# Operand distances for split products, and two more places for expert weights

## The chip, the cores and the metric

One core of one Trainium2 chip runs the whole program as one launch. The metric is the device time of that launch in microseconds, the median of several runs. TensorE multiplies, VectorE (DVE), ScalarE (ACT) and GpSimd (POOL) do the elementwise work, and SyncE (SP) issues nearly all large transfers from its queue, in order.

## The reference, cut to what matters

A network on 256 tokens of width 1024, all in float32. Three blocks follow one another: two layers of feed-forward and gated or pooling mixers (each layer has two SwiGLU feed-forwards of inner width 2816); an attention block (two kinds of heads side by side) with a mixture of 32 experts, each token going to 4 of them; and a block with attention and a scan, cross attention to a memory, and a feed-forward with a short convolution. The expert part is, with `h` the normalised tokens:

```python
logits = xf @ w_router + b_router            # 256 x 32
top_val, top_idx = lax.top_k(logits, 4)
gates = jax.nn.softmax(top_val, axis=-1)
hid = xb @ w_mlp1[e] + b_mlp1[e]             # rows of the tokens that chose e; 1024 x 2048
act = glu * sigmoid(1.702 * glu) * (lin + 1) # glu, lin: even and odd columns, clipped
y = act @ w_mlp2[e] + b_mlp2[e]              # 1024 x 1024, weighted by the gate and summed
```

The weights of one expert are 12 MB, those of all 32 are 384 MB.

## The kernel before

Activations lie transposed: `xT` is 128 partitions x 8 x 256, 8 KB in each partition.

**Split products.** Outside the experts a float32 product is made of three products of type fp32r. Each operand is split into a rounded part and the rest (`split`, `norm_parts`), and `mm3` issues high by high, high by low, low by high (L180, L181, L182). The weights, 128 x 128, are the stationary operand (in the profile `LDWEIGHTS`, engine PEld); the activations, 128 x 256, are the moving one. `xhi` and `xlo` hold the split input of a stage, two constant tiles of 8 KB a partition; `ahi`, `alo` (`yhi`, `mhi`, `so`, `ao`, `raw` elsewhere) are split intermediate activations. Split weights lie in tiles `hi` of a ring (`rings`, pool `splitp`, 4 or 8 tiles of 8 KB, high part then low part), in some stages with further tiles on the right side of the memory.

Where things lie follows from the order and the sizes of the pools. The constants begin at byte 16512 of each partition; `xT` is at 17088, `xhi` at 25280, `xlo` at 33472; then come `small`, `rawp` (ten slots of 8 KB for raw weights) from 55840, and the ring from 137760. Tiles inside an operand are multiples of 512 bytes, so what is left is the remainder of the addresses by 512:

| operand | remainder before | minus that of the weights, modulo 512 |
|---|---|---|
| weights in the ring `splitp` | 32 | |
| weights in the right ring (cross attention, convolution) | 480 | |
| `xhi`, `xlo` | 192 | 160 (224 to the right ring) |
| `ahi` of the four feed-forwards; `so`, `ao`, `mhi`; `raw` | 32 | 0 |
| `ahi` of the gated stage (`sgu`) | 64 | 32 |
| `ahi` of the pooling mixer, `yhi` of the cross attention, `ahi` of the convolution stage | 160 | 128 to `splitp`, 192 to the right ring |

**Experts.** `moe` takes the experts in an order that is partly known only after the routing. Expert 0 comes first, and its weights are loaded while the attention still runs. SP then reads the expert's number from `ids` (L1740) and issues 12 loads of 1 MB each (L1264), each into the next place of a fixed turn: 7 slots of `rawp`, 4 places of its own, 3 slots of `rawp`, 14 places. A load waits until the place's last reader is done, and everything behind it on SP's queue waits too.

The rows of the tokens that an expert wants are gathered by a product with a one-hot matrix. The tokens are split: `thi` and `tlo` lie in the memory of `xhi` and `xlo`, written by ACT (L1381) and, for the low part, by VectorE (`lows`, L1386, three pieces before the ranking of the experts and five behind it). Each gather multiplies both with the one-hot matrix `oh` (type fp32r): L1451 for expert 0, L1468 (`dispatch`, from `prepare`) for four places of the order at a time. `xT` stays in its constant tile, untouched, until `post_norm` adds the experts' output to it. Behind the last expert comes a loop for what did not fit (`For_i`, here run zero times), before which all engines meet at a barrier.

The program's order on TensorE is written out by hand in some stages (`in_order`); for the rest, and for SP's queue, a scheduler at build time orders instructions by priority and readiness.

## Time and profile before

| | us |
|---|---|
| median of 3 runs | 2688.53 (2688.33 to 2691.99) |
| the profiled execution, its own time | 2696.91 |
| its span, first to last instruction | 2695.2 |
| TensorE busy | 2443.8 (91%) |
| VectorE / ScalarE / GpSimd busy | 1343.3 / 918.1 / 254.0 |
| moved by DMA | 716.20 MB |

The profiled execution is 8.4 us slower than the median without the profiler. Durations of matrix products in the profile are modelled and overlap: the next one starts before the last has ended, so "busy" says that TensorE has work, not how fast it goes. The stages, by the trace: first feed-forward to 206 us, gated stage to 396, two feed-forwards to 597 and 754, pooling mixer to 850, feed-forward to 1036, attention to about 1196, experts to about 2187, attention and scan to 2400, cross attention to 2496, convolution stage to the end.

### The profile page before, as it was taken

What the parts mean: (1) busy time and instruction counts of PE and PEld (TensorE: products, weight loads), DVE (VectorE), ACT (ScalarE), POOL (GpSimd) and SP (SyncE); (2) the same over time, 40 slices, a digit from 0 to 9 for tenths busy, and PEclk for the clock granted to TensorE, in tenths of its full rate; (3) what the DMA queues carried; (4) which work ended last, traced back from release to release, by engine and by line L of the source; (5) the groups of instructions that cost most, each with busy time, mean ns of one, the idle gap of its engine ahead of it and who ended that gap; (6) DMA issues with size and microseconds to landing.
All of it is one profiled execution on the core that took longest, in us unless ns stands there. A gap on an engine that the chain in (4) does not pass through costs nothing. (4 is left out here: it accounts for less than half of the span.)

```text
span 2695.2 us, 42836 instructions
## 1 busy us (share of the span) xinstructions
PE 2443.8 (91%) x17207; PEld 1863.6 (69%) x17207; DVE 1343.3 (50%) x2786; ACT 918.1 (34%) x1531; POOL 254.0 (9%) x444
## 2 busy tenths in 40 slices
PE   7999999999999999999889888789777787999998
PEld 7998999999999998784333333223222156998997
DVE  5556677577777775942111111111111059766875
ACT  4445454454445444531100100001010042555653
POOL 0011000110021102220000000000000027111000
PEclk8999999999999999999989989899999798999999
DMA  7956455676737652449999999999999973444640
GB/s 240 325 181 201 158 195 196 211 254 219 235 126 266 207 178 97 142 183 367 419 413 420 416 415 418 420 420 419 420 419 419 419 268 110 157 162 136 218 142 17
DMA packets 274116, 716.20 MB, mean 266 GB/s; under 512 B 15023, under 2 KB 179354, under 8 KB 223610
## 3 DMA queue, kind: packets, MB, share of 16 engines
q1 hardware_dynamic: 269370, 703.63, 69.8%
q0 software_dynamic: 4544, 9.80, 1.1%
q8 instruction: 136, 2.23, 0.3%
q14 instruction: 66, 0.54, 0.1%
HBM read 703.84 MB, written 9.54 MB: 265 GB/s over the span
## 5 line engine op out<-in xcount | busy, mean ns | idle before, releaser
L182 PE MATMUL b<-xhi,hi 128*128 128x256 f32 x2392 | 681.5, 285 | 15.7 <-DVE hi L164 15.6
L180 PE MATMUL b<-xhi,hi 128*128 128x256 f32 x2392 | 685.9, 287 | 6.0 <-ACT xhi L192 4.9
L181 PE MATMUL b<-xlo,hi 128*128 128x256 f32 x2392 | 680.8, 285 | 4.6 <-DVE xlo L193 2.4
L164 DVE TENSOR_TENSOR hi<-raw,hi 128x1024 fp32r<-128x1024 f32 (+3 forms) x517 | 605.9, 1184 | 157.5 <-ACT hi L163 152.7
L163 ACT CAST hi<-raw 128x1024 fp32r<-128x1024 f32 (+3 forms) x517 | 509.7, 1003 | 510.4 <-PE b L182 458.4
L180 PEld LDWEIGHTS b<-xhi,hi 128*128 128x128 f32 x2392 | 460.3, 192 | 19.5 <-ACT hi L163 7.8
L182 PEld LDWEIGHTS b<-xhi,hi 128*128 128x128 f32 x2392 | 460.1, 192 | 18.2 <-DVE hi L164 18.0
L181 PEld LDWEIGHTS b<-xlo,hi 128*128 128x128 f32 x2392 | 460.3, 192 | 6.5 <-DVE xlo L193 4.5
L1477 DVE TENSOR_SCALAR g<-b 128x256 f32<-128x256 f32 x48 | 20.3, 422 | 596.1 <-PE b L1496 331.8
L180 PE MATMUL b<-ahi,hi 128*128 128x256 f32 x1072 | 303.4, 284 | 1.8 <-ACT ahi L163 1.7
L181 PE MATMUL b<-alo,hi 128*128 128x256 f32 x1072 | 302.3, 282 | 2.2 <-DVE alo L164 1.3
L182 PE MATMUL b<-ahi,hi 128*128 128x256 f32 x1072 | 301.7, 282 | 0.0
L181 PEld LDWEIGHTS b<-alo,hi 128*128 128x128 f32 x1072 | 203.4, 190 | 3.2 <-DVE alo L164 2.2
L180 PEld LDWEIGHTS b<-ahi,hi 128*128 128x128 f32 x1072 | 203.1, 190 | 3.0 <-ACT ahi L163 2.9
L182 PEld LDWEIGHTS b<-ahi,hi 128*128 128x128 f32 x1072 | 203.5, 190 | 0.0
L1480 ACT ACTIVATE sg<-g 128x256 f32<-128x256 f32 x48 | 20.0, 416 | 525.5 <-DVE g L1477 525.5
L1528 PE MATMUL b<-raw,xe 128*64 128x512 f32 x648 | 153.1, 609 | 16.6 <-DMA raw<-in_w_mlp_dram 16.6
L1496 PE MATMUL b<-raw,xe 128*32 128x512 f32 x928 | 124.9, 650 | 35.3 <-DMA raw<-in_w_mlp_dram 35.0
L1577 ACT COPY y<-b 64x512 f32<-64x512 f32 x68 | 39.4, 579 | 249.4 <-PE b L1570 241.6
L1528 PEld LDWEIGHTS b<-raw,xe 128*64 128x64 f32 x648 | 42.6, 138 | 118.1 <-issue 74.4
L452 DVE TENSOR_TENSOR t<-b,rb 128x256 f32<-128x256 f32 x88 | 37.1, 422 | 167.2 <-PE b L182 167.1
L1496 PEld LDWEIGHTS b<-raw,xe 128*32 128x32 f32 x928 | 24.1, 112 | 118.6 <-DMA raw<-in_w_mlp_dram 75.7
(662 smaller groups left out, 3278.7 us busy)
## 6 DMA issues: line engine op xcount, KB each, us to landing
raw<-in_w_mlp_dram SPq DMA_DIRECT2D x275, 1024.0 KB
wb<-in_w_mlp_dram SPq DMA_DIRECT2D x108, 1024.0 KB
raw<-in_ffn_w_in_dram SPq DMA_DIRECT2D x84, 1024.0 KB
raw<-in_ffn_w_out_dram SPq DMA_DIRECT2D x44, 1024.0 KB
raw<-in_w_ada_dram SPq DMA_DIRECT2D x24, 1024.0 KB
raw<-in_ffn_w_up_dram SPq DMA_DIRECT2D x22, 1024.0 KB
raw<-in_w_in_dram SPq DMA_DIRECT2D x21, 1024.0 KB
raw<-in_a_w_in_dram SPq DMA_DIRECT2D x16, 1024.0 KB
```

What stands on the lines that cost most here:

```text
L163: a = self.nc.scalar.copy(hi, src)
L164: return a.ins, self.nc.vector.tensor_tensor(lo, src, hi.bitcast(F32), op=ALU.subtract).ins
L180: mm(out, whi, xhi, start=start, stop=False, skip_group_check=True)
L181: mm(out, whi, xlo, start=False, stop=False, skip_group_check=True)
L182: mm(out, wlo, xhi, start=False, stop=stop, skip_group_check=True)
L452: nc.vector.tensor_tensor(t, ps[:, :T], rb, op=ALU.mult)
L1477: nc.vector.tensor_scalar(g, v[:, :, 0], 7.0, None, op0=ALU.min)
L1480: nc.scalar.activation(sg, g, AF.Sigmoid, scale=1.702)
L1496: mm(ps[32 * c:32 * c + 32, :], xe(k), chunk(w[k][:, 0, :], c), start=False, stop=k == KT - 1, tile_position=(0, 32 * c), skip_group_check ...
L1528: mm(pq[q][64 * b:64 * b + 64, :], xe(k), chunk(w[:, 0, :], 2 * q + b), start=False, stop=k == KT - 1, tile_position=(0, 64 * b), skip_gro ...
L1577: nc.scalar.copy(y[64 * z:64 * z + 64, 512 * c:512 * c + 512], py[64 * c:64 * c + 64, :])
```

## The change

**Distances.** `xhi` and `xlo` leave the constants and become tiles of a new pool `inputs` (two tiles of 8 KB) that stands between `rawp` and the ring; three small tiles (`b_route`, `fac`, `decay`, 320 bytes in all) go with them, and `sc` is made earlier. So `rawp` and `inputs` start at remainder 224, while the ring still starts at 137760. In the other pools a padding tile (`shift`) moves what follows it: by 192 bytes in the feed-forwards and in the mixing stage, 160 in the gated stage, 64 in the pooling, cross attention and convolution stages; 448 in the right ring. By the same reckoning of pools as above, the moving operands then lie at remainder 224 and the weights at 32 nearly everywhere, 192 above them modulo 512, or 320 counted from the other side. Unchanged are `cq` of the attention (32) and a product of the ring with itself (0); in the products of the gated stage whose moving operand is the weights, the distance goes from 352 to 320.

**Experts.** The tokens are kept as one float32 tile (`tokens`, in one tile of `inputs`) and the gathers are float32 products, half as many; `lows` is gone, the one-hot matrices are float32. `xT` is stored to DRAM (`kept`) at the beginning of the stage and loaded back behind the last expert's weights. The other tile of `inputs` and the tile of `xT` are lent to the weights: the turn is now 7 slots, 4 own, 2 lent, 3 slots, 16 places; the last expert of the order skips the lent ones.

```diff
+        self.inputs = pool("inputs", 2, reuse_waits="tile")
+        self.sc = self.const.tile([P, KT], F32, name="sc")
         self.xT = self.const.tile([P, KT, T], F32, name="xT")
-        self.xhi = self.const.tile([P, KT, T], F32R, name="xhi")
-        self.xlo = self.const.tile([P, KT, T], F32R, name="xlo")
+        self.new_inputs()
...
+                if side == "right":
+                    self.shifts[more] = 448
+    def shift(self, pool, n):
+        pool.tile([P, n // 4], F32, tag="shift", name=self.nm("shift"), bufs=1)
+    def input(self, dtype=F32):
+        return self.inputs.tile([P, KT * T], dtype, tag="input", name=self.nm("input"))
+    def new_inputs(self):
+        self.xhi, self.xlo = (self.input(F32R).rearrange("p (j t) -> p j t", j=KT) for _ in range(2))
...
         with self.tc.tile_pool(name=self.nm("ffna"), bufs=3) as ap_:
+            self.shift(ap_, 192)
...
-        places = itertools.cycle([self.slot] * 7 + [own] * 4 + [self.slot] * 3)
-        place = lambda: next(places)()
+        lent = [self.input, lambda: self.xT.rearrange("p j t -> p (j t)")]
+        places = itertools.cycle([self.slot] * 7 + [own] * 4 + lent + [self.slot] * 3)
+        def place(last=False):
+            p = next(places)
+            return next(q for q in itertools.chain([p], places) if not (last and q in lent))()
...
+        nc.sync.dma_start(self.kept, self.xT)
         b1 = pb.tile([P, 2, 512], F32R, name=self.nm("b1"))
...
-            nc.scalar.activation(thi[:, h, :, s], src, AF.Identity, scale=r2[:, h:h + 1])
-        def lows(some, last):
-            with self.behind(last):
-                for h, s, src in some:
-                    x = nc.vector.scalar_tensor_tensor(tlo[:, h, :, s], src, r2[:, h:h + 1], thi[:, h, :, s].bitcast(F32), op0=ALU.mult, op1=ALU.subtract)
-            return [x.ins]
-        last = lows(turned[:3], [last])
+            nc.scalar.activation(tokens[:, h, :, s], src, AF.Identity, scale=r2[:, h:h + 1])
...
-            for i, t in enumerate((thi, tlo)):
-                for k in range(4):
-                    o = ps[k // 2][:, k % 2, :]
-                    for h in range(2):
-                        mm(o, t[:, h, some + k, :], oh0[:, h, :], start=i == 0 and k % 2 == 0 and h == 0, stop=i == 1 and h == 1, skip_group_check=True)
-                fill()
+            for k in range(4):
+                o = ps[k // 2][:, k % 2, :]
+                for h in range(2):
+                    mm(o, tokens[:, h, some + k, :], oh0[:, h, :], start=k % 2 == 0 and h == 0, stop=h == 1, skip_group_check=True)
+            fill()
...
-                        for i, (t, h) in enumerate(((thi, 0), (thi, 1), (tlo, 0), (tlo, 1))):
-                            mm(o, t[:, h, k + z, :], oh[:, h, :], start=z == 0 and i == 0, stop=i == 3, skip_group_check=True)
+                        for h in range(2):
+                            mm(o, tokens[:, h, k + z, :], oh[:, h, :], start=z == 0 and h == 0, stop=h == 1, skip_group_check=True)
...
+            nc.sync.dma_start(self.xT, self.kept)
             units = self.first_units(*ahead.pop(0)) if ahead else None
...
         outer_pools.close()
+        self.new_inputs()
```

## Rows read from the trace of the kernel before

**Rows 1.** The page's busy times over the whole span, and two stretches (the third of the four feed-forward stages, the expert stage): the stretch and its length, then for each engine its busy us and (x instructions) for PE, PEld, DVE, ACT, POOL, then the granted TensorE clock (1.00 is 2.4 GHz, 0.50 is 1.2 GHz), the DMA engines' mean busy share and the GB/s moved.

```profile
PE 2443.8 (91%) x17207; PEld 1863.6 (69%) x17207; DVE 1343.3 (50%) x2786; ACT 918.1 (34%) x1531; POOL 254.0 (9%) x444
...
597.00:754.00 157.00, 157.00 (x1329) 152.71 (x1328) 116.80 (x314) 70.96 (x96) 11.07 (x46) 1.00 0.64 212
...
1196.00:2187.00 991.00, 817.37 (x4301) 314.71 (x4300) 158.87 (x494) 102.43 (x205) 9.23 (x40) 0.91 0.99 407
```

**Rows 2.** Groups of instructions by line, over the whole span, those of L180 with 256 moving columns (L181 and L182 have the same counts): line, engine, operation, out<-in by the names (moving operand, then weights), shapes, xcount | busy us, mean ns of one | idle before.

```profile
L180 PE MATMUL b<-xhi,hi 128*128 128x256 f32 x2392 | 685.9, 287 | 6.0 <-ACT xhi L192 4.9 <-ACT xhi L912 1.1
L180 PE MATMUL b<-ahi,hi 128*128 128x256 f32 x1072 | 303.4, 284 | 1.8 <-ACT ahi L163 1.7
...
L180 PE MATMUL b<-raw,hi 128*128 128x256 f32 x72 | 21.0, 292 | 2.1 <-ACT hi L163 1.2 <-ACT raw L163 1.0
L180 PE MATMUL b<-yhi,hi 128*128 128x256 f32 x64 | 18.3, 286 | 0.0
L180 PE MATMUL b<-mhi,hi 128*128 128x256 f32 x64 | 18.2, 285 | 0.0
L180 PE MATMUL b<-so,hi 128*128 128x256 f32 x32 | 9.6, 300 | 0.3 <-ACT so L163 0.3
L180 PE MATMUL b<-ao,hi 128*128 128x256 f32 x32 | 9.3, 291 | 0.0
```

**Rows 3.** The products with the tile `ahi` alone, in three stretches (gated stage, pooling mixer, convolution stage): after the length, busy us and (x products) of PE, then PEld, DVE, ACT, the clock, the DMA share, GB/s.

```profile
206.00:396.00 190.00, 58.18 (x307) 48.01 (x306) 8.06 (x19) 7.71 (x19) 0.98 0.56 185
...
754.00:850.00 96.00, 32.39 (x176) 27.45 (x176) 4.35 (x10) 4.46 (x10) 0.98 0.60 203
...
2496.00:2696.00 200.00, 65.96 (x352) 55.37 (x352) 9.28 (x22) 8.93 (x22) 0.97 0.36 121
```

**Rows 4.** The timeline of TensorE: start in us, duration in us, engine, line, operation, names, shapes. Of each run of split products without a pause the first and the last start stand here; the number of steps between them is 23 (distance 0, third feed-forward), 17 (distance 160, same stage), 20 (distance 32, gated stage), 11 (distance 128, convolution stage, weights in `splitp`), 20 (distance 192, convolution stage, weights in the right ring), 21 (distance 192, cross attention: the first of nine such runs in the trace) and 22 (distance 192, convolution stage: the last of the nine).

```profile
628.41 0.28 PE L180 MATMUL b<-ahi,hi 128*128 128x256 f32 x1
...
631.16 0.28 PE L182 MATMUL b<-ahi,hi 128*128 128x256 f32 x1
...
604.00 0.28 PE L180 MATMUL b<-xhi,hi 128*128 128x256 f32 x1
...
606.00 0.28 PE L182 MATMUL b<-xhi,hi 128*128 128x256 f32 x1
...
333.59 0.28 PE L180 MATMUL b<-ahi,hi 128*128 128x256 f32 x1
...
335.93 0.28 PE L182 MATMUL b<-ahi,hi 128*128 128x256 f32 x1
...
2601.48 0.28 PE L180 MATMUL b<-ahi,hi 128*128 128x256 f32 x1
...
2602.79 0.28 PE L182 MATMUL b<-ahi,hi 128*128 128x256 f32 x1
...
2514.76 0.28 PE L180 MATMUL b<-ahi,hi 128*128 128x256 f32 x1
...
2517.03 0.28 PE L182 MATMUL b<-ahi,hi 128*128 128x256 f32 x1
...
2449.68 0.28 PE L181 MATMUL b<-ylo,hi 128*128 128x256 f32 x1
...
2452.15 0.28 PE L181 MATMUL b<-ylo,hi 128*128 128x256 f32 x1
...
2659.63 0.28 PE L181 MATMUL b<-alo,hi 128*128 128x256 f32 x1
...
2662.22 0.28 PE L182 MATMUL b<-ahi,hi 128*128 128x256 f32 x1
```

**Rows 5.** Three stretches around the beginning of the expert stage (columns as in rows 1), and SP's queue in the timeline: first issue in us, time from there to the end of the last issue, line, tile<-source, xcount.

```profile
1190.00:1195.00 5.00, 4.59 (x44) 4.48 (x44) 3.81 (x5) 2.52 (x12) 4.42 (x3) 1.00 0.18 61
1204.00:1247.00 43.00, 41.24 (x201) 23.48 (x203) 15.46 (x66) 7.43 (x14) 0.61 (x1) 0.84 0.80 301
1247.00:2165.00 918.00, 757.19 (x4004) 275.82 (x4000) 129.13 (x389) 81.08 (x162) 2.05 (x3) 0.91 1.01 417
...
1204.38 5.47 SPq L1264 DMA_DIRECT2D raw<-in_w_mlp_dram  x3
...
1219.08 13.34 SPq L1264 DMA_DIRECT2D raw<-in_w_mlp_dram  x7
...
2128.47 17.79 SPq L1264 DMA_DIRECT2D raw<-in_w_mlp_dram  x8
```

**Rows 6.** Groups by line (columns as in rows 2): the low parts of the tokens on VectorE and half of the gather of expert 0, from 1190 to 1245 us; and, over the whole span, a float32 product of 256 columns (L2564, each product two records).

```profile
L1386 DVE SCALAR_TENSOR_TENSOR xlo<-b,r,xhi 128x256 fp32r<-128x256 f32 x8 | 3.3, 476 | 0.9 <-ACT xhi L1381 0.9
...
L1451 PE MATMUL b<-oh,xhi 128*128 128x64 f32 x16 | 3.1, 346 | 0.2 <-DVE oh L1424 0.2
...
L2564 PE MATMUL b<-raw,m2f 128*128 128x256 f32 x128 | 31.0, 399 | 9.2 <-ACT sq L1185 5.6 <-DMA raw<-in_xa_wv_dram 3.7
```

**Rows 7.** The timeline at the end of the expert stage, for TensorE, SP's queue and ACT (in brackets the idle time before and what ended it): the last expert's last products, the issue of the next stage's first weights, ACT's last splits of them and its first instruction behind the barrier of the loop.

```profile
2165.86 1.06 PE L1570 MATMUL b<-raw,aTh 128*32 128x512 f32 x8 [1.02 <-DMA raw<-in_w_mlp_dram]
...
2148.38 13.93 SPq L300 DMA_DIRECT2D raw<-in_w_in_dram  x2
...
2171.81 1.99 ACT L163 CAST hi<-raw 128x1024 fp32r<-128x1024 f32 x2 [0.91 <-issue]
...
2175.26 1.08 ACT L1185 ACTIVATE sq<-b 128x512 f32<-128x512 f32 x2 [1.46 <-SPq L1760]
```

## The prediction

> **What bounds the kernel now.** I read the stages first. The page and its stretches [rows 1] show two kernels in one: before 1196 us and after 2187 us TensorE is busy almost without a gap (157.00 of 157.00 us in the third feed-forward stage), with the DMA engines at 0.64; in between, in the expert stage, TensorE is busy for 817 of 991 us and the DMA share is 0.99. So the first thing the change touches, the pace of the split products, pays in the first and last part, and the second, the places for weights, in the middle.

> Then I read the pace. "Busy" says nothing of it, since the modelled durations overlap (280 ns each); what counts is the time from one start to the next in the timeline. [Rows 4] holds runs of split products in which nothing waits, first and last start of each. By the distances that the memory map gives (moving operand minus weights, modulo 512):

> - 0 (feed-forward activations): 23 steps in 2.75 us, 119.6 ns
> - 160 (`xhi`, `xlo`): 17 steps in 2.00 us, 117.6 ns
> - 32 (gated stage): 20 steps in 2.34 us, 117.0 ns
> - 128 (convolution stage, ring on the left): 11 steps in 1.31 us, 119.1 ns
> - 192, which is 320 from the other side (ring on the right, whose weights start at 480): 20 steps in 2.27 us, 113.5 ns; but in another such run 21 steps in 2.47 us, 117.6 ns, and in a third 22 in 2.59 us, 117.7 ns

> The same 256 columns with the same 128 columns of weights, at the same clock: the pace follows the distance. Distance 192 is where the change puts nearly everything, and the trace has it already: nine undisturbed runs, of which the first, the last and one between stand there. Four go at about 113.5 ns and five at about 117.7, and a run that has settled stays at its level. That is the uncertainty of this forecast.

> **The split products.** The count is that of [rows 2], three lines of the helper for each, so three times the printed number. The level after I take as four ninths of 113.5 and five ninths of 117.7: 115.8 ns.

> - `xhi`, `xlo`: 3 x 2392 = 7176 at 117.6, 1.8 ns less each: 12.9 us
> - activations `ahi`, `alo`: 3 x 1072 = 3216. By [rows 3] (hi parts alone; the lo parts are half as many) 307 x 1.5 = 461 are of the gated stage, 264 of the pooling stage, 528 of the convolution; 1964 are left for the four feed-forward stages. Those: 3.8 ns each, 7.5 us. Gated: 1.2 ns, 0.6 us. Pooling, and the 192 `yhi` of the cross attention, at distance 128: 456 x 3.3 ns, 1.5 us. Convolution: half are at 192 now, the other 264 give 0.9 us
> - `raw`, `mhi`, `so`, `ao`, all at distance 0: 3 x 200 = 600 at 3.8 ns, 2.3 us

> Together 25.7 us. About a tenth of these products stand in the attentions and the scan (1036 to 1196, 2187 to 2298, 2400 to 2496 us), where TensorE also waits for others; I count half of those, so 0.95 x 25.7 = 24.4 us. Bounds: all at 113.5 ns gives 29.4 + 12.0 + 1.6 + 2.6 + 2.1 + 3.7 = 51.4, times 0.95, 48.8 us; all at 117.7 gives 4.3 x 0.95 = 4.1 us. The 240 products of 512 columns get distance 320 instead of 352, which no row prices; at a few ns either way they are under 1 us. The padding tiles carry no instructions. What is next after TensorE in these stages, VectorE, is busy 1343 us in all [rows 1], far from taking over for one per cent.

> [...]

> **The expert stage.** It ends when its weights have come: the last product waits for a landing [rows 7], and from 1247 to 2165 us the DMA share is 1.01 at 417 GB/s, against 0.80 from 1204 to 1247 [rows 5]. So a gain is what starts the full stream earlier, a loss what is put into it.

> - Two more places. The ids are known at about 1204; then three loads go (places still free), the next only at 1219.08, when expert 0's products release places. With the two lent places first in the turn, five go at once and every later one two places earlier, as long as releases and not the DMA set the pace, which is until 1247. One load is worth 2.49 us (eight issues in 17.79 us at full stream, seven steps): 2 x 2.49 = 5.0 us gained. At least 0, if the places come free late; the lent ones were last read by the attention and the router, both over by 1196.
> - The gather of expert 0, which those releases wait for: 16 + 16 fp32r products become 16 float32 ones, and eight subtractions on VectorE (L1386, 0.48 us each) go [rows 6]. Float32 products appear as two records each; 128 of 256 columns take 31.0 us, 242 ns a record. At 64 columns I have no row: between nothing and that price scaled by columns the gather gets up to 3.5 us shorter. The next gather (192 columns, 32 records) grows: 32 x 182 = 5.8 us against 32 x 117 ns = 3.7 us by the pace of [rows 4], 2.1 us later. These two oppose each other; I take 0, bounds -3.5 and +2.1.
> - The later gathers, eight of 32 records: 16 x 484 ns = 7.7 us for 32 x 0.118 = 3.8 us, 3.9 us each, 31 us of TensorE. What hides them is the 174 us in which TensorE is idle there (991 - 817), and 14 to 16 loads in flight, about 35 us of stream, against a delay of 4. I cost them at 0; without that cover they are the rival that is slower.
> - The store of `xT` (1 MB) comes when the stream stands nearly still: 61 GB/s from 1190 to 1195 [rows 5]. It stands on SP's queue, in order, before loads of expert 0 that are wanted 20 to 40 us later. 0, bound +2.5 us.
> - The load back stands on SP's queue behind the last expert's weights and ahead of the next stage's first two weights, whose second landing I take to be what ACT's last splits wait for until 2171.81, just before the barrier of the loop, behind which ACT goes on at 2175.26 [rows 7]. One more MB ahead of it: +2.5 us; 0 if it is put behind.

> Sum: -5.0 + 0 + 0 + 0 + 2.5 = -2.5 us, between -8.5 and +7.1.

> **The total.** -24.4 - 2.5 = -26.9 us. The rows are of a profiled execution of 2696.91 us (span 2695.2), 8.4 us over the median of the unprofiled runs, 2688.53; I subtract from the median: 2661.6, so 2661.5 us.

> **Rivals.**

> A, the forecast: the levels at distance 192 stay mixed, 114.5 to 117.0 ns on average, 2650 to 2675 us. For it: nine runs, four and five. Chance 0.55.

> B, the fast level holds. With one distance everywhere nothing throws a run off it. Price 48.8 + 2.5: 2637 us. Against: five of nine runs did not find it, and each wait starts anew. 0.19.

> C, the slow level holds: 4.1 + 2.5, 2682 us. For: it is the commoner of the two, and the last run of [rows 4], which follows `xhi` products without a pause, stays there for all its products. 0.14, half of it within 0.2% if the expert stage gives nothing.

> D, the distance does not matter and the paces of [rows 4] come from something else in those stages (their banks, their neighbours). Then only the expert stage moves: 2686 us. Against: 128 and 192 stand in one stage, with moving tiles of the same pool and only the weights on another side. 0.06.

> E, TensorE becomes the pace of the expert stage through the float32 gathers, at its eight later gathers. [...] It decides once TensorE's wait for weights between two gathers (four slots) falls under 4 us and the loads in flight are used up. Against: 174 us of idle TensorE. 0.06.

> About 0.2% (5.4 us) is what a measurement of this kernel can tell from no change. Faster: A, B and half of C, 0.81; within: half of C and D, 0.13; slower: E, 0.06. For 8 in 10 the range reaches to B and past C with the expert stage's upper bound: 2637 to 2685 us.

> **What would show it.** Right: starts of `xhi` and `ahi` products 113 to 118 ns apart in every stage, `ahi` of the feed-forward no longer at 119.6; feed-forward stages about 1.5% shorter each; five loads issued at once after the ids, the full stream some 5 us earlier relative to them; the load of `xT` between the last weights and the next stage's. Wrong: paces unchanged at new distances (D); one level alone (B, C); DMA share under 1 in the expert stage with TensorE waiting for nothing (E); SP standing at the store or the load of `xT` while places are free.

## The result and the profile after

The changed kernel takes 2649.86 us (median of 4 runs, 2645.62 to 2650.19) against 2689.06 us: a ratio of 0.9849, 95% interval 0.9836 to 0.9861, 39 us less. The forecast was 2661.5, 27 us less, in a range of 2637 to 2685: the direction and the mechanism held, the size of one term did not. Its profiled execution took 2649.92 us (span 2648.2).

In what follows a pace is the mean time from one start of a split product of 256 columns to the next, over all neighbours less than 160 ns apart, so without waits and at the upper clock level (granted clock 1.00; at the lower one, 0.50, the starts stand 213 to 214 ns apart, as 16 of them do from 796.2 to 799.2 us of the changed kernel). The clock stands here as a share of full speed, as the page gives it; no run shows it in GHz, as the line of [rows 1] has it.

The page of the changed kernel, and the same two stretches as in [rows 1] (its third feed-forward stage, its expert stage):

```profile
PE 2416.1 (91%) x17207; PEld 1833.3 (69%) x17207; DVE 1339.3 (51%) x2778; ACT 915.4 (35%) x1531; POOL 254.3 (10%) x444
...
578.40:729.60 151.20, 151.20 (x1329) 147.64 (x1331) 116.51 (x314) 70.19 (x98) 11.10 (x46) 1.00 0.67 222
1162.74:2150.19 987.45, 836.01 (x4301) 331.29 (x4300) 156.77 (x486) 103.16 (x205) 9.27 (x40) 0.91 1.00 410
```

The same 1329 products of the feed-forward stage now need 151.2 us instead of 157.0, still without a gap and at the same clock. The expert stage is 3.5 us shorter, its TensorE 19 us busier. Placing each of the 11,586 split products of the one trace beside the same product of the other, the changed kernel is 33.3 us ahead where the expert stage begins, 36.8 us at the first product behind it, and 47 us at the end. (The profiled execution of before was a long one; experiment 7 comes back to that.)

The timeline of TensorE in the changed kernel, a place in its second feed-forward stage that shows both levels (columns as in [rows 4]; `input` is `xhi` or `xlo`). The first and the last start of a run of 19 steps, a group of other products, and the first and the last start of a run of 32 steps:

```profile
565.33 0.28 PE L199 MATMUL b<-input,hi 128*128 128x256 f32 x1
...
567.56 0.28 PE L200 MATMUL b<-input,hi 128*128 128x256 f32 x1
567.68 0.95 PE L274 MATMUL b<-ones,sums 128*128 128x1 f32 x8
568.49 0.36 PE L198 MATMUL b<-input,hi 128*128 128x256 f32 x1
...
568.81 0.28 PE L200 MATMUL b<-input,hi 128*128 128x256 f32 x1
...
572.44 0.28 PE L199 MATMUL b<-input,hi 128*128 128x256 f32 x1
```

2.23 us by 19 steps are 117.4 ns, 3.63 by 32 are 113.4: same tiles, same distance, and the level changes at the interruption. Over the whole trace the 10,756 neighbours at distance 192 have a pace of 114.5 ns. They form 97 stretches of at least 14 products without an interruption; behind their first steps 66 stand at 113.3 ns and 31 at 117.8, none between and none that changes on the way. By products that is 76% at the fast level; the forecast took four ninths.

SP's queue at the beginning and at the end of the expert stage (columns as in [rows 5]; the ids are there at 1170.10 us, in the kernel before at 1203.32):

```profile
1158.54 0.33 SPq L1342 DMA_DIRECT2D kept<-xT  x1
1162.87 0.32 SPq L1344 DMA_DIRECT2D b<-b  x1
1163.23 0.42 SPq L1294 DMA_DIRECT2D wb<-in_w_mlp_dram  x1
...
1171.10 0.36 SPq L1294 DMA_DIRECT2D input<-in_w_mlp_dram  x1
1171.71 0.34 SPq L1294 DMA_DIRECT2D xT<-in_w_mlp_dram  x1
1172.30 26.88 SPq L1294 DMA_DIRECT2D raw<-in_w_mlp_dram  x10
...
2100.66 7.83 SPq L1294 DMA_DIRECT2D raw<-in_w_mlp_dram  x4
2110.54 0.33 SPq L1776 DMA_DIRECT2D xT<-kept  x1
2113.09 13.31 SPq L318 DMA_DIRECT2D raw<-in_w_in_dram  x2
2126.49 4.01 SPq L318 DMA_DIRECT2D raw<-in_xa_wv_dram  x1
2141.20 0.35 SPq L2089 DMA_DIRECT2D raw<-tab  x1
```

From the ids to the issue of the last weights it is now 938.05 us, before 942.61: 4.56 us less. From there to SP's first issue behind the loop (`tab`) it is 33.05 us, before 30.71: 2.34 us more.

### The profile page after: what moved, and what is told of

Same layout as the page of the kernel before. It is cut to its first block, busy times and chain, and to the rows that moved or that the text cites. A ratio compares the mean times of both kernels' runs of the same rounds, so it can differ in the third digit from the quotient of the medians.

```text
span 2648.2 us, 42809 instructions
## 1 busy us (share of the span) xinstructions
PE 2416.1 (91%) x17207; PEld 1833.3 (69%) x17207; DVE 1339.3 (51%) x2778; ACT 915.4 (35%) x1531; POOL 254.3 (10%) x444
## 3 DMA queue, kind: packets, MB, share of 16 engines
q8 instruction: 136, 2.23, 0.3%
## 5 line engine op out<-in xcount | busy, mean ns | idle before, releaser
L200 PE MATMUL b<-input,hi 128*128 128x256 f32 x2392 | 671.6, 281 | 16.2 <-DVE hi L182 16.1
L198 PE MATMUL b<-input,hi 128*128 128x256 f32 x2392 | 675.5, 282 | 6.4 <-ACT input L210 5.1
L182 DVE TENSOR_TENSOR hi<-raw,hi 128x1024 fp32r<-128x1024 f32 (+3 forms) x517 | 605.8, 1183 | 146.4 <-ACT hi L181 145.5
L199 PE MATMUL b<-input,hi 128*128 128x256 f32 x2392 | 670.6, 280 | 3.7 <-DVE input L211 2.4
L181 ACT CAST hi<-raw 128x1024 fp32r<-128x1024 f32 (+3 forms) x517 | 509.0, 1002 | 469.4 <-PE b L200 408.2
L198 PEld LDWEIGHTS b<-input,hi 128*128 128x128 f32 x2392 | 456.4, 191 | 20.1 <-ACT hi L181 7.2
L200 PEld LDWEIGHTS b<-input,hi 128*128 128x128 f32 x2392 | 455.4, 190 | 18.9 <-DVE hi L182 18.8
L199 PEld LDWEIGHTS b<-input,hi 128*128 128x128 f32 x2392 | 456.0, 191 | 5.8 <-DVE input L211 4.5
L198 PE MATMUL b<-ahi,hi 128*128 128x256 f32 x1072 | 299.2, 280 | 2.2 <-ACT ahi L181 2.2
L200 PE MATMUL b<-ahi,hi 128*128 128x256 f32 x1072 | 297.5, 278 | 0.8 <-DVE hi L182 0.8
L1548 PE MATMUL b<-raw,xe 128*64 128x512 f32 x600 | 140.9, 607 | 10.2 <-DMA raw<-in_w_mlp_dram 10.1
L1516 PE MATMUL b<-raw,xe 128*32 128x512 f32 x784 | 107.9, 660 | 32.9 <-DMA raw<-in_w_mlp_dram 32.9
```

What stands on the lines that cost most here:

```text
L181: a = self.nc.scalar.copy(hi, src)
L182: return a.ins, self.nc.vector.tensor_tensor(lo, src, hi.bitcast(F32), op=ALU.subtract).ins
L198: mm(out, whi, xhi, start=start, stop=False, skip_group_check=True)
L199: mm(out, whi, xlo, start=False, stop=False, skip_group_check=True)
L200: mm(out, wlo, xhi, start=False, stop=stop, skip_group_check=True)
L1516: mm(ps[32 * c:32 * c + 32, :], xe(k), chunk(w[k][:, 0, :], c), start=False, stop=k == KT - 1, tile_position=(0, 32 * c), skip_group_check ...
```

## The experiments

The times of before beside them are those of runs taken together with them, 2689 to 2690 us.

**1. The distances alone, and the places alone.** Two kernels that split the change. The first keeps the pools and paddings of the change and takes the expert stage from the kernel before. The second is the changed kernel with the paddings so set that every product has its old distance, at new addresses:

```diff
-            self.shift(ap_, 192)        (and the five like it)
-                    self.shifts[more] = 448
+                    self.shifts[more] = 320
...
+        self.shift(self.inputs, 160)
         self.new_inputs()
+        self.inputs.tile([P, 8], F32, tag="pad", name="pad", bufs=1)
```

Distances alone:

> The distances of the changed kernel with the expert stage of the kernel before (split tokens, no lent places, no store or load of `xT`). Theory: the split products carry nearly all of the change, and the expert stage only the 2.2 us that its loads show (weights done 4.56 us earlier after the ids, the load of `xT` 2.34 us later). So 2649.9 + 2.2 = 2652 us, between 2650 and 2655. Rival: the 12 us by which the result passed the forecast come from the expert stage or from the two parts together; then about 2662 us, as the forecast's sum for the distances alone, 2689 - 24.4 = 2664.6, says. If the distance does not matter: 2689 us.

Measured: 2652.1 us (2648.42 to 2655.23), ratio 0.9863 (0.9846 to 0.9879). Places alone:

> The expert stage of the changed kernel with every split product at the distance of the kernel before (the addresses themselves all differ, the differences modulo 512 are the old ones, product by product). Theory: 2689.1 - 2.2 = 2687 us, between 2684 and 2689, and paces of 119.7 ns at distance 0, 117.9 at 160, 116.8 at 32, since the difference counts and not the address. Rival: the places are worth the 12 us by which the result passed the forecast: 2675 us. If addresses count and not differences, the paces come out as in neither kernel.

Measured: 2688.47 us (2682.86 to 2693.84, 10 runs), ratio 0.9992 (0.9982 to 1.0001). So the distances carry 37.3 us and the expert stage 0.9, with an interval from nothing to 5. The paces of the second kernel are those of the kernel before, distance by distance: 119.71 ns at 0, 117.84 at 160, 116.76 at 32, 118.54 at 128 (before 119.72, 117.89, 116.77, 118.62), though every address has another remainder. The difference counts, not the address.

**2. A program of nothing but split products.**

> Another program: it copies x to the output, and its only other work are split products as in the kernel (256 columns, 128 weight columns, high, high, low), 96 to a run, with one set of weights and sixteen moving tiles that stand 0, 32, 64 ... 480 bytes from it modulo 512; each distance has a run in each of two orders, and 192, 320, 64 and 192 a longer run at the end. It computes nothing of the reference. Theory: the spacing of starts depends on the distance alone: 119.7 ns at 0, 116.8 at 32, 118.6 at 128, 117.3 to 119 at 160, 118 at 224, 113.3 or 117.8 at 192, and the same in both orders but for 192. Whether one of the ten distances that the kernels do not have is better than 192 is open. [...]

The probe's timeline of TensorE: start, time from there to the end of the last product, and in the name of the moving tile its distance. The duration of the last one is 0.28 us, so a pace is (time - 0.28) by 95:

```profile
55.34 11.06 PE L71 MATMUL b<-x192e,w 128*128 128x256 f32 x96
66.23 11.67 PE L71 MATMUL b<-x352e,w 128*128 128x256 f32 x96
77.74 11.56 PE L71 MATMUL b<-x128e,w 128*128 128x256 f32 x96
...
100.50 11.37 PE L71 MATMUL b<-x32e,w 128*128 128x256 f32 x96
111.70 11.47 PE L71 MATMUL b<-x320e,w 128*128 128x256 f32 x96
123.01 11.68 PE L71 MATMUL b<-x256e,w 128*128 128x256 f32 x96
134.52 11.47 PE L71 MATMUL b<-x64e,w 128*128 128x256 f32 x96
145.83 11.47 PE L71 MATMUL b<-x448e,w 128*128 128x256 f32 x96
...
293.62 11.06 PE L71 MATMUL b<-x448e,w 128*128 128x256 f32 x96
304.52 11.47 PE L71 MATMUL b<-x64e,w 128*128 128x256 f32 x96
...
395.01 11.66 PE L71 MATMUL b<-x0e,w 128*128 128x256 f32 x96
406.51 32.82 PE L71 MATMUL b<-x192e,w 128*128 128x256 f32 x288
439.17 34.08 PE L71 MATMUL b<-x320e,w 128*128 128x256 f32 x288
```

192 gives 10.78 by 95, 113.5 ns; 0 gives 119.8, 256 gives 120.0, 352 gives 119.9. The products, their weights and their order are the same in all rows; only the place of the moving tile against the weights differs, and it is worth up to 6 ns per product. If the distance did not matter, as rival D has it, all rows would be alike. Two things were new. Distances that differ by 256 have the same levels: 0 and 256, and 96 and 352 too, all stand at 119.8 to 120.0, 128 and 384 at 118.6 to 118.7, 224 and 480 at 118.3 (one row each of 160 and 288 stands 1.3 and 1.1 ns off that of the distance 256 away). And 448 shows both levels of 192, 117.8 ns the first time and 113.5 the second, while 64 and 320, as far apart from the other side, stand at 117.8 in all six runs.

**3. The same with interruptions, to count the draws.**

> As the probe, with other distances (steps of 16 and 8 bytes among them) and a break behind every 24 products: the next group waits until VectorE has read the bank, by copies of different lengths, 14 groups to a distance. It computes nothing of the reference. Theory, a group keeps the level it starts at and a start at 192 finds the fast one in about seven of ten (66 of 96 stretches of 14 products or more in the changed kernel): about 10 of the 14 groups at 113.3 ns, the others at 117.8, none between; 64 and 320 all at 117.8; 448 as 192. Rival, the level is drawn for a distance once and for all: all 14 alike. Whether 176, 184, 200 or 208 do better than 192 is open.

The groups of 24 at distance 192 that end before 70 us, and two each of 64 and 448 (in brackets the wait for VectorE ahead of each):

```profile
49.52 3.00 PE L74 MATMUL b<-x192e,w 128*128 128x256 f32 x24 [0.32 <-DVE seen L76]
52.86 3.09 PE L74 MATMUL b<-x192e,w 128*128 128x256 f32 x24 [0.33 <-DVE seen L76]
56.31 3.01 PE L74 MATMUL b<-x192e,w 128*128 128x256 f32 x24 [0.35 <-DVE seen L76]
59.68 3.01 PE L74 MATMUL b<-x192e,w 128*128 128x256 f32 x24 [0.37 <-DVE seen L76]
63.08 3.09 PE L74 MATMUL b<-x192e,w 128*128 128x256 f32 x24 [0.38 <-DVE seen L76]
...
97.42 3.10 PE L74 MATMUL b<-x64e,w 128*128 128x256 f32 x24 [0.32 <-DVE seen L76]
100.86 3.09 PE L74 MATMUL b<-x64e,w 128*128 128x256 f32 x24 [0.33 <-DVE seen L76]
...
198.28 3.00 PE L74 MATMUL b<-x448e,w 128*128 128x256 f32 x24 [0.34 <-DVE seen L76]
201.64 3.09 PE L74 MATMUL b<-x448e,w 128*128 128x256 f32 x24 [0.35 <-DVE seen L76]
```

At 192 and 448 a group takes 2.99 to 3.01 us or 3.09, nothing between, and the next start draws anew: 12 of 14 groups fast at 192 (the first of them has no wait ahead of it), 12 of 14 at 448, none of 14 at 64, one of 14 at 320. A fast group need not start fast: behind the first step of 0.22 us that every group has, up to four steps of up to 124 ns come, and then it stays at 113.3.

Of the other distances only 112 comes to 113.3 ns in every group. The 114.1 to 115.2 ns that are given for it below are means of short groups with such a beginning in them: behind the first step come six to ten of 113 to 121 ns, and the last twelve steps of each of the 14 groups are 113.3 ns. So 112 found the fast level at every one of these starts, which 192 doesn't. Whether it stays there over hundreds of products, and what it would be worth in the kernel, no run shows; the tiles of this kernel stand at multiples of 32 bytes, and 112 isn't one.

A last probe went on around it:

> As the second probe, with the distances that are odd multiples of 8 bytes, and 108 and 116, around 112, which had no slow level (114.1 to 115.2 ns in all 14 groups). It computes nothing of the reference. Open is whether a distance holds 113.3 ns or less in every group. If none does, a kernel whose tiles stand at multiples of 32 bytes has no distance better than 192 and 448.

All of these are slower: between 117.8 and 122.3 ns in every group (without its first four steps), 121.8 on average at 116 and 120. 112 is a single good distance between bad ones.

**4. Other distances in the kernel itself.** The padding is set so that the 11,187 products have 64, or 0, instead of 192; for 0:

```diff
         self.new_inputs()
+        self.shift(self.inputs, 192)
...
-                    self.shifts[more] = 448
+                    self.shifts[more] = 256
```

(and the paddings of the stage pools to match).

> The changed kernel with the weights 128 bytes further on, so that the distance is 64 (modulo 512) at the same 11,187 products that have 192 now; all else stays. In the probe 64 and 320 stood at 117.8 ns in all six runs, 192 at 113.3 in all five. Theory, it counts which operand lies ahead: 11,187 x (117.8 - 114.5) = 37 us more, 2687 us. Rival, only the gap of 64 bytes modulo 256 counts, from whichever side: the same as the changed kernel, 2650 us.

(192 has four runs in the probe, not five.) Measured: 2681.51 us (2674.26 to 2686.16, 6 runs), ratio 0.9960 (0.9944 to 0.9976). The pace is 117.6 ns, 90 of 95 stretches slow. One of the 90 began fast: 17 steps at 113.3 ns, then 117.8 to its end, without an interruption between.

> The changed kernel with all these products at distance 0. Theory, the distance alone sets the pace and nothing else of the change does: 119.7 ns against 114.5, 11,187 x 5.2 = 58 us more, 2708 us. Rival, what the change moved (where the operands lie at all, another order of the pools) gave part of the gain: clearly under 2700 us.

Measured: 2703.19 us (2702.74 to 2703.40). The pace is 119.9 ns. With all else of the change in place, this kernel is slower than the kernel before, ratio 1.0049 (1.0030 to 1.0069): the distance is the cause of the gain, and it can be turned into a loss. Both came out a little under their forecasts, 32 us over the changed kernel instead of 37, and 53 instead of 58. The paces would give 3.14 ns x 11,187 = 35 us and 5.45 ns x 11,187 = 61: 0.90 and 0.87 of what the pace loses reaches the end. For the distances alone it is 4.03 ns (118.26 in the kernel before, 114.23 with the distances alone, over all products) x 11,340 products of 256 columns = 46 us of pace for 37.3 us of time, 0.82, and by the interval of that time 0.71 to 0.91.

**5. One place lent, or none.**

> The changed kernel with one lent place, that of the second operand; `xT` is not lent, so it is neither stored nor loaded back. Theory: half of the 4.56 us of earlier loads goes (2.3 us), and the 2.34 us of the load back come again: the same as the changed kernel, 2649.9 us, between 2648 and 2652. Rival: the store and the load cost nothing that shows: 2652 us or more.

Measured: 2651.56 us (2648.22 to 2656.05), which the spread can't tell from the changed kernel. By the loads: 941.07 us from the ids to the last weights, and 30.71 from there to the loop's end.

> The changed kernel with the tokens' rows in float32 but neither place lent (and so no store or load of `xT`): what the float32 gathers alone do to the expert stage, read from the loads. Theory: nothing; the last weights are issued 942.6 to 943.7 us after the ids, as in the two runs with split tokens, and the first issue behind the loop's barrier comes 30.7 us later. Rival, the gather of expert 0 got shorter or the later ones longer in a way that the stream shows: 940 or less, or 946 or more.

Measured, in one run of 2655.88 us: 944.25 us and 30.70. The kernels with split tokens have 942.61, 943.11 (before, second profile) and 943.68 (distances alone), so what the float32 gathers do by themselves is 1.1 us on average, as much as these three differ among themselves. From no place to one is 3.2 us, from one to two 2.0 (the six kernels with two lie between 937.91 and 940.75, mean 939.1).

**6. The load back of `xT` at another place.** First behind the next stage's weights:

```diff
-            nc.sync.dma_start(self.xT, self.kept)
             units = self.first_units(*ahead.pop(0)) if ahead else None
             if mem:
                 mem.fetch("v", 3)
+            nc.sync.dma_start(self.xT, self.kept)
```

> The changed kernel with the load back of `xT` issued behind the next stage's first two weights and the memory's value weights, not ahead of them. Theory, these are what the barrier behind the expert stage waits for, and the megabyte ahead of them costs the 2.34 us seen there: 2649.9 - 2.3 = 2647.6 us, and in the trace the first issue behind the barrier comes 30.7 us after the last weights' instead of 33.1. Rival: `xT` is wanted at once behind the barrier and the wait only moves: 2650 us.

Measured: 2653.7 us (2646.53 to 2656.28). SP's queue:

```profile
2099.04 7.82 SPq L1294 DMA_DIRECT2D raw<-in_w_mlp_dram  x4
2108.96 13.63 SPq L318 DMA_DIRECT2D raw<-in_w_in_dram  x2
2122.68 3.74 SPq L318 DMA_DIRECT2D raw<-in_xa_wv_dram  x1
2126.47 2.85 SPq L1779 DMA_DIRECT2D xT<-kept  x1
2139.69 0.35 SPq L2089 DMA_DIRECT2D raw<-tab  x1
```

The last weights are issued at 2106.53 here, so it is 33.16 us to `tab`: nothing gained. Wherever the load stands ahead of the loop, the loop's end comes 33.0 to 33.2 us after the last weights (five kernels), and without it there 30.7 (five others), so the barrier ahead of the loop waits for it too. The first split products of the mixing stage even start 44.3 us after the last weights here, against 42.2 in the changed kernel. Then behind the loop:

> The changed kernel with the load back of `xT` issued behind the loop, first on SP's queue there. Theory, the barrier ahead of the loop waits for all that was issued before it, so the load must leave that side: 30.7 us from the last weights' issue to the barrier's end instead of 33.0, while the residual sum needs `xT` only 8 us behind the barrier; 2649.9 - 2.3 = 2647.6 us, which the spread of the executions (some 4 us to either side) hides, so the trace decides. Rival: the wait moves to the residual sum, or to the weights and tables that come behind it in the queue, and the first products of the mixing stage start as late as before.

```profile
2122.99 3.74 SPq L318 DMA_DIRECT2D raw<-in_xa_wv_dram  x1
2137.46 0.35 SPq L1811 DMA_DIRECT2D xT<-kept  x1
2137.85 0.43 SPq L2089 DMA_DIRECT2D raw<-tab  x1
```

Measured: 2651.55 us (2649.49 to 2654.41). The loop's end comes 30.62 us after the last weights (2106.84), as expected; but the residual sum starts 9.2 us behind it, not 8.2, and the mixing stage's first split products 40.9 us after the last weights, against those 42.2. Of the 2.4 us 1.0 goes to a new wait, and the 1.4 that are left don't show in the time.

**7. The kernel before, once more.**

> The kernel before once more, with a second profiled execution. The spans of the two profiles differ by 47.0 us and the medians by 39.2, because the first profiled execution of the kernel before (2696.91 us) lies 8 us over the median of its runs; 5.5 us of it can be the attention's output stretch, 36.1 us at a granted clock of 0.86, against 30.6 us at 1.00 in the changed kernel. Theory, that was one draw among many: the second profiled execution lies between 2683 and 2694 us, where the unprofiled ones lie, and has that stretch at 1.00 or the paces at distance 160 lower. Rival, a profile lengthens this kernel: 2696 to 2697 us again, with the same clock and paces.

Measured: 2691.09 us (2686.7 to 2694.26, 10 runs); the profiled execution took 2692.78 us, 4.1 less than the first, at a clock of 0.95 in about that stretch. The paces are the same to 0.03 ns at the distances 0 and 160, four fifths of all products. The 4.1 us come from elsewhere. In the gated stage it is 1.5 us, where waits are shorter. In the attention's output stretch it is 2.7 us, and there it is the clock: 46 products stand about 213 ns apart in the first profile (granted clock 0.86), 18 in the second (0.95), and 5 in the changed kernel (1.00). So the 47 us between the first pair of profiles hold about 4 us of an unlucky execution, and 42.9 us is the difference of the spans with the second.

## Why the prediction was right, and where its size was off

**The bound and the mechanism were right.** The split products' pace is set by the distance (experiments 1, 2 and 4), the expert stage by its stream of weights. Rival D, no effect of the distance, fell in every one of these runs. Without such an effect the probe's rows would all be alike; they stand between 113.5 and 120.0 ns.

**The step that was mis-sized is the level after, 115.8 ns.** It came from nine runs, four fast and five slow [rows 4]. In the changed kernel 76% of the products stand at the fast level and the pace is 114.5. The forecast's sum counts about 10,900 products at the new distance, so 1.3 ns are 14 us more than its 25.7, and the mean of 117.89 for `xhi` and `xlo` instead of the 117.6 of one run is 2 more: 42. Times what reaches the end by experiment 4, 0.82, that is 34 us, where the distances alone gave 37.3. The factor of 0.95 was too high by the same comparison (0.82 to 0.90), but this error was the smaller and went the other way.

Why nine runs misled: they all stand in the last two stages, and a second profile of the kernel before gives four of nine again, with some of the places changed. With 31 starts of 97 slow, as in the changed kernel, five or more slow of nine come up about once in eight times, so the sample was somewhat unlucky. What chooses the level at a start is open. It is not the length of the wait alone: in the second probe's rows a wait of 0.35 us leads to a fast group at 192 and to a slow one at 448.

**Rivals B and C.** Neither level holds everywhere. At 192 a run that has settled does stay, as the prediction said; B's argument that nothing throws it off was wrong at the interruptions, behind which either level followed (66 and 31 of the 97 stretches). The measured time lies by the edge of A, 2650 to 2675, on B's side. C's picture, the slow level nearly everywhere, is what distance 64 does: 2681.5 us, against C's 2682.

**The expert stage came out as forecast, by its terms.** Two more places: 5.0 forecast, 4.56 in the pair of traces, 5.2 between none and two. The gathers 0: 0.6 to 1.6 us, and expert 0's products release their first place 15.75 us after the ids as before (15.76). The load of `xT` +2.5: 2.34, and it was the barrier that paid. Sum -2.5: ids to loop's end 971.10 us instead of 973.32, -2.2. (The rest of the 3.5 us of the stage lies behind the loop, where the second profile of the kernel before is 0.9 us shorter too.) One sign was wrong: not five loads went at once after the ids but three, and two more almost 7 us later. The "three loads" of the kernel before were misread in the same way: the first went 1.06 us after the ids, the other two at 5.62 and 6.20.

The store of `xT` was costed at 0, with the remark that SP might stand at it. It did: 11.7 us until `xT` was whole and 3.9 at the bias behind it, and the fourth load of expert 0's second weights went out 6.9 us ahead of the ids instead of 23.3. It costs nothing because that load is wanted only 40 us later, where the places come free [rows 5].

**Rival E** stayed away as argued. The float32 gathers' products mostly start 0.216 us apart instead of 0.118, TensorE is busy 19 us more in the stage (31 were forecast), and the DMA share stays at 1.00.

## What to carry to other kernels

Read the pace of products from start to start in stretches without waits, and lay the addresses of the two operands beside it: in these runs the pace followed the difference of the two, and a few bytes of padding were worth up to 4.5% of every product (119.9 ns against 114.5). Measure the distances in a probe of their own before choosing one, with many starts each, since a distance can have two levels, as 192 has here (113.3 and 117.8 ns), and the trace at hand may show too few starts to tell their shares, as nine did here, and with runs as long as those of the kernel, since a group of 24 products is partly its own beginning (at 112 its first seven to eleven steps). And where a load is moved out of a barrier's way, read from the trace what the barrier waits for: here the loop's end came 33.0 to 33.2 us after the last weights at both places of the load ahead of the barrier, and 30.6 us with the load behind it.
